# Sparse attention, first half of the queries: float32 weights and values in place of high and low parts

## Chip, cores and metric

One core of a Trainium2 chip runs the whole kernel as one program. The metric is the device time of one execution in microseconds (us). The time of a kernel is the median of its runs.

## The reference, cut to what is touched

The reference is two transformer layers over 1024 tokens of width 1024. Layer 0 mixes with gated linear attention and latent attention, layer 1 with a sparse attention and a state-space model (S5); each layer ends in a squared-ReLU network. The change touches the last lines of the sparse attention:

```python
def _dsa(q, k, v, q_idx, k_idx, w_idx):        # 8 heads of 64, 1024 tokens
    ...
    def one_block(args):                        # 128 queries at a time
        ...
        _, sel = lax.top_k(score, topk)         # 256 keys for each query
        sel_ok = sel <= qpos[None, :, None]
        ...
        s = jnp.where(sel_ok[:, None], s, -jnp.inf)
        p = jax.nn.softmax(s, axis=-1)
        return jnp.einsum('bhqk,bqkhd->bhqd', p, v_sel)
```

The kernel computes it densely: a bias row of 0 or a large negative number (`bias[qb]`) takes out the keys that are not chosen, and the weights `p` of all keys up to the query are multiplied with the values.

## The kernel before, in words

**Order of the work.** The kernel is written as a plain sequence of operations (`program`, line 2161) that a planner, `Plan`, records and then orders itself. `Plan.order` (line 242) is a list scheduler with its own table of costs (`cost`, line 207): at each moment it gives each free engine the ready operation with the smallest key, where the key is the place in the written sequence less a number called `rush`. It also places all SBUF and PSUM tiles. The result is a fixed order for each engine. Every instruction has line 471 in the profile, so it is told apart by its tiles. A changed operation anywhere can change the order of everything that is planned at about the same time or later.

**High and low parts.** Most products are made of operands that are split in two: `split` (line 580) writes a rounded copy (type `fp32r`, the high part) by a ScalarE copy, and the rest (low part) by a subtraction on VectorE or GpSimd. `mm3` then multiplies high by high, high by low and low by high. `fp32r` operands are multiplied in one pass. Some small products of the kernel are multiplied in plain float32.

**The layer around the change.** After the network of layer 0 the program calls, woven into each other: the index scores and the search for the 256th largest score (`index`, `topk`, lines 1587 and 1616, VectorE and ScalarE), the projections of layer 1 (`l1_in`, line 1699, TensorE), the S5 (`s5`, all engines), and the sparse attention `dsa` (line 1753) for the first 512 queries (h = 0) and then for the last 512 (h = 1). After them come the output projection and the network, dense work for TensorE.

**Values.** In `l1_in` eight tiles of 128 tokens by 512 value columns are made in PSUM. Each is split, for each of two groups of four heads, into a tile in which a head has 128 columns, high and low part beside each other: for an even head high first, for an odd head low first. So 4 ScalarE copies of 128 columns and 4 VectorE subtractions a tile, and two writes to the DRAM buffer `dv`. `dsa` loads those it needs back through GpSimd's queue: for h = 0 four tiles for each group of heads.

**Weights times values.** `attention` (line 1015) goes through heads and pairs of query blocks. `first` makes the scores, and exponentials in `p` with ScalarE. `second` takes pairs of key blocks (`kb`): up to four 128x128 transposes of `p` into one PSUM tile `pt`, a ScalarE copy to `hi` (tile `pth`), a VectorE subtraction to `lo` (tile `ptl`), and four matmuls into the accumulator:

```python
v = value(kb + a)                     # 128 columns: high and low part of one head
TE.matmul(o, v, hi[:, c], ...)        # c: 256 query columns
TE.matmul(o, v, lo[:, c], ...)
```

On the diagonal (`kb == qa`) the quarter that lies above it is cleared in both tiles by a memset (VectorE here, `ZE = 1`) and not transposed. The accumulator then has 128 rows: 64 from the values' high part, 64 from their low part. `fold` (line 1083) adds the two: a ScalarE copy of one half to the rows of the other (tile `fold`), and a VectorE addition into `og`. For h = 0 a head has three pairs of key blocks, two of them on the diagonal. The latent attention of layer 0 uses the same two functions.

Of the kernel before, what the change touches and what calls it, by code (L numbers as in the profile page):

```python
# [11 lines left out]
F32 = mybir.dt.float32  # L12
# [504 lines left out]
class Kern:  # L517
# [497 lines left out]
    def attention(self, items):  # L1015
# [27 lines left out]
        def second(i, pr, pp):  # L1043
            hd, h, _, _, value, emit = items[i]
            qa = h * 4 + pr * 2
            if pr == 0:
                acc[i] = self.ps1()
            o = acc[i][:, pr * 256:pr * 256 + 256]
            for kb in range(0, qa + 2, 2):
                self.nc.rush += self.DS  # L1050

                pt = self.ps1((P, 2, 2, P))
                hi, lo = self.slab(F32R, "pth"), self.slab(F32R, "ptl")
                off = P if kb == qa else 0
                for z in (hi, lo):
                    if off:
                        (self.ZE or G).memset(z[:, :off].bitcast(F32), 0.0)
                        self.nc.after(pp[2])
                for a in range(2):
                    for j in range(2):  # L1060
                        if kb + a <= qa + j:
                            TE.transpose(pt[:, 1 - a, j, :], pp[j][:, (kb + a) * P:(kb + a + 1) * P], self.identf)
                self.split(pt.rearrange("p a b c -> p (a b c)")[:, off:], hi[:, off:], lo[:, off:], S, V)
                for a in range(2):
                    v = value(kb + a)
                    c = slice(256 - a * 256, 512 - a * 256)
                    TE.matmul(o, v, hi[:, c], start=kb + a == 0, stop=False)
                    TE.matmul(o, v, lo[:, c], start=False, stop=kb + a == qa + 1)
                self.nc.rush -= self.DS
            if pr == 1:  # L1070
                emit(acc.pop(i), sums[hd // 2, h])
# [11 lines left out]
    def fold(self, po, odd, og, sums):  # L1083
# [4 lines left out]
        tmp = self.slab(name="fold")  # L1088
        self.copy(self.S, tmp[own], po[other])
        V.tensor_tensor(og[own], po[own], tmp[own], ALU.add)  # L1090
# [608 lines left out]
    def l1_in(self, x, dq, dk, dv, du):  # L1699
# [4 lines left out]
        for b in range(8):  # L1704
# [3 lines left out]
            for hg in range(2):  # L1708
# [6 lines left out]
                nc.scalar.dma_start(out=dv[b, hg], in_=v.rearrange("p a b c -> p (a b c)").bitcast(F32))  # L1715
# [37 lines left out]
    def dsa(self, dq, dk, dv, bias, mix, h):  # L1753
# [3 lines left out]
        ld = G.dma_start  # L1757

        def load(pr):

            if pr % 2 == 0:
                for b in range(4 * h + 4):
                    v = self.slab(F32R, "vv")
                    ld(out=v, in_=dv[b, pr // 2])
                    val[pr // 2, b] = v
# [9 lines left out]
        def item(hd):  # L1775
# [19 lines left out]
            def emit(po, sums):  # L1795
                if not odd:
                    og[h] = self.slab(name="og")
                self.fold(po, odd, og[h], sums)
# [6 lines left out]
            return hd, h, prep, score, lambda kb: val[hd // 4, kb][:, (hd % 4) * P:(hd % 4 + 1) * P], emit  # L1805

        yield from self.attention([item(hd) for hd in range(8)])
# [327 lines left out]
BY = {'unit_h': 'S', 'unit_l': 'E', 'loadx_h': 'S', 'loadx_l': 'V', 'glao_h': 'S', 'glao_l': 'G', 'mlac_h': 'S', 'mlac_l': 'V', 'mlaq_h': 'S', 'mlaq_l': 'G', 'mlao_h': 'S', 'mlao_l': 'E', 'half_h': 'S', 'half_l': 'V', 'fc1_h': 'S', 'fc1_l': 'E', 'dsao_h': 'S', 'dsao_l': 'G', 'x2_h': 'H', 'x2_l': 'V', 'y_h': 'H', 'y_l': 'G', 'glu_h': 'H', 'glu_l': 'V', 'lnacc': 'G', 'lnsq': 'G', 'gla': 'G', 'gdl': 'G', 'gor': 'G', 's5u': 'V', 's5a': 'G', 's5m': 'G', 's5n': 'G', 's5t': 'G', 's5g': 'G', 'lo16': 'V', 'hi16': 'V'}  # L2135
BACK, SQUARE = 1, 1   
# [24 lines left out]
def program(K, A, out, stop=None):  # L2161
# [23 lines left out]
    dv = K.dram("dv", [8, 2, P, N])  # L2185
# [211 lines left out]
```

## Time and profile before

| what | value |
|---|---|
| median of 3 runs | 2381.92 us (2379.25 to 2382.75) |
| profiled execution, its own time | 2390.38 us |
| span in that profile | 2388.6 us, 33377 instructions |
| busy: TensorE / weight loads / VectorE / ScalarE / GpSimd | 2305.8 / 1910.2 / 1768.3 / 1330.8 / 468.2 us |
| mean granted TensorE clock | 0.99 |

How to read it: PE is TensorE's matmuls and PEld its weight loads, DVE is VectorE, ACT is ScalarE, POOL is GpSimd, SP only issues DMAs. A matmul's form is given as rows*columns of the weights and the shape of the moving operand; a plain float32 matmul leaves two such records. A record lasts from its issue until its results are out, and the next one starts before that, so the step from start to start is what it costs an engine that has enough to do.

### The profile page before, as it was taken

To read this page: it belongs to the slowest core of one execution; us is meant where nothing else is said; L and a number is where in the kernel's file an instruction comes from. 1 tells how busy PE (TensorE), PEld (TensorE's weight loads), DVE (VectorE), ACT (ScalarE), POOL (GpSimd) and SP (SyncE) were. 2 spreads that over 40 slices of the span, in tenths; PEclk is the share of its full clock that TensorE was granted. 3 is DMA by queue.
4 is the path that set the end of the run, shared out by engine and by line. 5 is a ranking of instruction groups with operands and counts; after the bars stand their busy time and mean duration, and the time that the engine had idled before them with its cause. 6 is when DMAs were issued, how large, how long until landed. Compare 5 with 4: busy or idle time off the path is not lost. (4 is left out here: it accounts for less than half of the span.)

```text
span 2388.6 us, 33377 instructions
## 1 busy us (share of the span) xinstructions
PE 2305.8 (97%) x11368; PEld 1910.2 (80%) x11368; DVE 1768.3 (74%) x3353; ACT 1330.8 (56%) x2648; POOL 468.2 (20%) x488
## 2 busy tenths in 40 slices
PE   8999999999999999999999997899999999999997
PEld 7788888887878788887778876788877787888887
DVE  8676778468776567579799989885587755675796
ACT  4365567437555554446578775775275455444463
POOL 1252332232000000003211235752320000000021
PEclk9999999999999999999999998999999999999998
DMA  5420001325654585655103469553155546665561
GB/s 182 170 80 1 1 1 51 101 71 162 204 168 154 190 299 194 207 189 203 67 36 115 145 204 282 155 157 127 53 166 187 168 146 212 225 253 193 178 238 36
DMA packets 174939, 356.59 MB, mean 149 GB/s; under 512 B 26784, under 2 KB 39344, under 8 KB 174768
## 3 DMA queue, kind: packets, MB, share of 16 engines
q1 hardware_dynamic: 110704, 243.81, 31.9%
q10 hardware_dynamic: 51392, 87.58, 9.9%
q0 software_dynamic: 12672, 23.07, 3.6%
q8 instruction: 89, 1.46, 0.3%
q14 instruction: 82, 0.67, 0.1%
HBM read 249.66 MB, written 104.73 MB: 148 GB/s over the span
## 5 line engine op out<-in xcount | busy, mean ns | idle before, releaser
L471 PE MATMUL PS<-bh,wb 128*128 128x512 f32 x1792 | 569.0, 395 | 14.5 <-ACT u L471 6.8
L471 PEld LDWEIGHTS PS<-bh,wb 128*128 128x128 f32 x1792 | 335.6, 188 | 105.1 <-ACT u L471 12.6
L471 PE MATMUL PS<-bl,wb 128*128 128x512 f32 x896 | 350.5, 391 | 0.0
L471 PE MATMUL PS<-gl,vh 128*128 128x512 f32 x832 | 324.0, 390 | 2.1 <-DVE gl L471 2.1
L471 PE MATMUL PS<-gh,vh 128*128 128x512 f32 x832 | 322.6, 391 | 2.5 <-ACT vh L471 1.8
L471 PE MATMUL PS<-gh,vl 128*128 128x512 f32 x832 | 323.7, 390 | 0.0
L471 PEld LDWEIGHTS PS<-bl,wb 128*128 128x128 f32 x896 | 169.2, 189 | 34.1
L471 PEld LDWEIGHTS PS<-gh,vh 128*128 128x128 f32 x832 | 156.1, 188 | 37.5 <-ACT vh L471 2.2
L471 PEld LDWEIGHTS PS<-gl,vh 128*128 128x128 f32 x832 | 156.2, 188 | 35.2 <-DVE gl L471 2.5
L471 PEld LDWEIGHTS PS<-gh,vl 128*128 128x128 f32 x832 | 156.2, 188 | 32.3
L471 POOL TENSOR_TENSOR wl<-wr,wh 128x512 fp32r<-128x512 f32 x77 | 120.8, 1584 | 254.9 <-ACT wh L471 154.4
L471 ACT ACTIVATE c<-c 128x512 f32<-128x512 f32 x224 | 140.7, 630 | 50.5 <-DVE c L471 43.5
L471 PE MATMUL PS<-xh,wh 128*128 128x512 f32 (+1 forms) x400 | 155.2, 393 | 12.7 <-ACT xh L471 6.7
L471 POOL TENSOR_TENSOR lnacc<-res,res 128x512 f32<-128x512 f32 (+1 forms) x8 | 9.8, 1223 | 768.1 <-DVE res L471 740.9
L471 ACT ACTIVATE gh<-hr 128x512 fp32r<-128x512 f32 x208 | 129.2, 623 | 52.1 <-PE PS L471 32.6
L471 PE MATMUL PS<-xh,wl 128*128 128x512 f32 (+1 forms) x400 | 154.1, 388 | 2.8 <-POOL wl L471 2.8
L471 DVE TENSOR_TENSOR gl<-hr,gh 128x512 fp32r<-128x512 f32 x208 | 147.7, 711 | 10.9 <-PE PS L471 5.2
L471 PE MATMUL PS<-xl,wh 128*128 128x512 f32 (+1 forms) x400 | 155.3, 389 | 0.0
L471 ACT ACTIVATE wb<-wf 128x512 fp32r<-128x512 f32 x96 | 59.7, 628 | 153.2 <-DMA wf<-in_l_w 94.0
L471 DVE TENSOR_TENSOR wb<-s,wb 128x512 fp32r<-128x512 f32 x128 | 87.8, 688 | 77.0 <-ACT wb L471 76.9
L471 DVE TENSOR_TENSOR vl<-s,vh 128x512 fp32r<-128x512 f32 x112 | 84.2, 754 | 78.5 <-ACT vh L471 39.9
L471 ACT ACTIVATE vh<-s 128x512 fp32r<-128x512 f32 x112 | 70.2, 629 | 108.3 <-PE PS L471 73.2
(371 smaller groups left out, 5497.5 us busy)
## 6 DMA issues: line engine op xcount, KB each, us to landing
wr<-in_l_w SPq DMA_DIRECT2D x118, 512.0 KB, 5.3
hr<-hd SPq DMA_DIRECT2D x208, 256.0 KB, 3.4
wf<-in_l_w SPq DMA_DIRECT2D x80, 512.0 KB, 3.8
hd<-t ACTq DMA_DIRECT2D x128, 256.0 KB, 2.7
hd<-c ACTq DMA_DIRECT2D x96, 256.0 KB, 2.3
wr<-in_l_fm SPq DMA_DIRECT2D x25, 512.0 KB, 5.3
wr<-in_l_wo SPq DMA_DIRECT2D x16, 512.0 KB, 4.5
dx<-res ACTq DMA_DIRECT2D x32, 256.0 KB, 2.4
```

The source lines that it names most:

```text
L471: r = getattr(queue.real, method)(*a, **k)
```

## The change

For the first half of the queries (`PLAIN = 0,`) the weights are copied once to a float32 tile and multiplied with float32 values of 64 columns. The accumulator uses only the head's own 64 rows, so that `fold` is one copy. On the diagonal nothing is cleared; the second matmul covers only the 128 columns below. The value tiles of the first four token blocks are written a second time, whole and in float32; `dv` gets another shape. The second half and the latent attention of layer 0 stay as they are.

```diff
--- before.py
+++ after.py
@@ -1012,7 +1012,8 @@
         output(*late)
-    def attention(self, items):
+    def attention(self, items, plain=False):
+
@@ -1046,20 +1047,28 @@
             if pr == 0:
                 acc[i] = self.ps1()
             o = acc[i][:, pr * 256:pr * 256 + 256]
+            if plain:
+                o = o[64 * (hd % 2):64 * (hd % 2) + 64]
             for kb in range(0, qa + 2, 2):
                 self.nc.rush += self.DS
                 pt = self.ps1((P, 2, 2, P))
-                hi, lo = self.slab(F32R, "pth"), self.slab(F32R, "ptl")
+                hi, lo = (self.slab(name="pt"), None) if plain else (self.slab(F32R, "pth"), self.slab(F32R, "ptl"))
                 off = P if kb == qa else 0
                 for z in (hi, lo):
-                    if off:
+                    if off and not plain:
                         (self.ZE or G).memset(z[:, :off].bitcast(F32), 0.0)
                         self.nc.after(pp[2])
                 for a in range(2):
                     for j in range(2):
                         if kb + a <= qa + j:
                             TE.transpose(pt[:, 1 - a, j, :], pp[j][:, (kb + a) * P:(kb + a + 1) * P], self.identf)
+                if plain:
+                    self.copy(S, hi[:, off:], pt.rearrange("p a b c -> p (a b c)")[:, off:])
+                    TE.matmul(o, value(kb), hi[:, 256:], start=kb == 0, stop=kb == qa)
+                    TE.matmul(o[:, off:], value(kb + 1), hi[:, off:256], start=False, stop=kb == qa, skip_group_check=off > 0)
+                    self.nc.rush -= self.DS
+                    continue
                 self.split(pt.rearrange("p a b c -> p (a b c)")[:, off:], hi[:, off:], lo[:, off:], S, V)
                 for a in range(2):
                     v = value(kb + a)
@@ -1080,14 +1089,17 @@
             ahead = nxt
             yield
-    def fold(self, po, odd, og, sums):
+    def fold(self, po, odd, og, sums, plain=False):
         V = self.V
         own, other = (slice(64, 128), slice(0, 64)) if odd else (slice(0, 64), slice(64, 128))
-        tmp = self.slab(name="fold")
-        self.copy(self.S, tmp[own], po[other])
-        V.tensor_tensor(og[own], po[own], tmp[own], ALU.add)
+        if plain:
+            self.copy(self.S, og[own], po[own])
+        else:
+            tmp = self.slab(name="fold")
+            self.copy(self.S, tmp[own], po[other])
+            V.tensor_tensor(og[own], po[own], tmp[own], ALU.add)
         if odd:
             V.reciprocal(sums, sums)
             rs, ps = self.slab(name="rs", shape=(P, 8, 64)), self.ps1()
@@ -1705,14 +1717,18 @@
             ps = self.ps1((P, 8, 64))
             bs = slice((b % 4) * P, (b % 4 + 1) * P)
             self.tm(us, lambda k: tuple(t[:, bs] for t in x[k][b // 4]), ps)
-            for hg in range(2):
+            if 1 in PLAIN or 0 in PLAIN and b < 4:
+                v = self.slab(name="vv")
+                self.copy(S, v, ps.rearrange("p a b -> p (a b)"))
+                nc.scalar.dma_start(out=dv[2, b], in_=v)
+            for hg in range(2 if len(PLAIN) < 2 and (b < 4 or 1 not in PLAIN) else 0):
                 v = self.slab(F32R, "vv", (P, 4, 2, 64))
                 for par in range(2):
                     src = ps[:, hg * 4 + par:hg * 4 + 4:2, :]
                     hs, ls = v[:, par::2, par, :], v[:, par::2, 1 - par, :]
                     self.copy(S, hs, src)
                     V.tensor_tensor(ls, src, hs, ALU.subtract)
-                nc.scalar.dma_start(out=dv[b, hg], in_=v.rearrange("p a b c -> p (a b c)").bitcast(F32))
+                nc.scalar.dma_start(out=dv[hg, b], in_=v.rearrange("p a b c -> p (a b c)").bitcast(F32))
             yield
         us = [self.unit(A["l1_u"][i]) for i in range(4)]
         for h in range(2):
@@ -1754,14 +1770,18 @@
         V, S, G, TE = self.V, self.S, self.G, self.TE
         val, qk, og = {}, {}, {}
-        ld = G.dma_start
+        ld, plain = G.dma_start, h in PLAIN
         def load(pr):
-            if pr % 2 == 0:
+            if plain and pr == 0:
+                for b in range(4 * h + 4):
+                    val[b] = self.slab(name="vv")
+                    ld(out=val[b], in_=dv[2, b])
+            elif not plain and pr % 2 == 0:
                 for b in range(4 * h + 4):
                     v = self.slab(F32R, "vv")
-                    ld(out=v, in_=dv[b, pr // 2])
+                    ld(out=v, in_=dv[pr // 2, b])
                     val[pr // 2, b] = v
             for odd in range(2):
                 q = self.slab(F32R, "qa")
@@ -1795,16 +1815,19 @@
             def emit(po, sums):
                 if not odd:
                     og[h] = self.slab(name="og")
-                self.fold(po, odd, og[h], sums)
+                self.fold(po, odd, og[h], sums, plain)
                 if odd:
                     self.dump("o_dsa", og[h], (pr, slice(None), slice(h * N, h * N + N)))
                     hi, lo = self.slab(F32R, "mh"), self.slab(F32R, "ml")
                     self.split(og[h], hi, lo, self.by("dsao_h"), self.by("dsao_l"))
                     mix[pr][h] = (hi, lo)
-            return hd, h, prep, score, lambda kb: val[hd // 4, kb][:, (hd % 4) * P:(hd % 4 + 1) * P], emit
-
-        yield from self.attention([item(hd) for hd in range(8)])
+            def value(kb):
+                return val[kb][:, hd * 64:hd * 64 + 64] if plain else val[hd // 4, kb][:, (hd % 4) * P:(hd % 4 + 1) * P]
+
+            return hd, h, prep, score, value, emit
+
+        yield from self.attention([item(hd) for hd in range(8)], plain)
     def turn(self, a, n):
@@ -2133,6 +2156,7 @@
+PLAIN = 0,
 BACK, SQUARE = 1, 1
 EARLY, ER = 100, 2
 FIRST = 3
@@ -2182,7 +2206,7 @@
     dr = K.dram("dr", [KD, P, T])
     dq = K.dram("dq", [4, 2, 2, P, N])
     dk = K.dram("dk", [4, 2, 2, 2, P, N])
-    dv = K.dram("dv", [8, 2, P, N])
+    dv = K.dram("dv", [3, 8, P, N])
     du = K.dram("du", [4, 2, P, N])
```

## Rows read from the trace of the kernel before

**Rows 1.** The page, part 1: busy time of TensorE and VectorE.
```profile
PE 2305.8 (97%) x11368; PEld 1910.2 (80%) x11368; DVE 1768.3 (74%) x3353; ACT 1330.8 (56%) x2648; POOL 468.2 (20%) x488
```

**Rows 2.** Busy time by stage, with the columns in the first row.
```profile
core 0: us, PE busy (x) PEld busy (x) DVE busy (x) ACT busy (x) POOL busy (x), PEclk, DMA share, GB/s
...
1250.00:1290.00 40.00, 38.46 (x170) 31.31 (x169) 39.58 (x94) 27.83 (x66) 5.15 (x4) 1.00 0.26 93
...
1467.00:1540.00 73.00, 61.66 (x403) 51.53 (x401) 65.58 (x186) 57.71 (x141) 53.34 (x62) 0.95 0.67 186
1540.00:1645.00 105.00, 102.62 (x661) 89.50 (x661) 95.63 (x242) 88.02 (x170) 49.97 (x58) 1.00 0.57 166
2089.00:2149.00 60.00, 60.00 (x267) 49.67 (x266) 45.39 (x71) 27.62 (x48) 4.54 (x3) 1.00 0.68 254
```

**Rows 3.** Matmuls from 2089 to 2149, by form: busy us, mean ns of one.
```profile
L471 PE MATMUL PS<-gl,vh 128*128 128x512 f32 x89 | 34.6, 389 | 0.0
```

**Rows 4.** TensorE in order of time, steps from start to start, from 1502 to 1506.
```profile
1502.34 0.39 PE L471 MATMUL PS<-s5T,s5U 128*128 128x128 f32 x2
1502.56 0.39 PE L471 MATMUL PS<-s5tab,s5x 128*128 128x128 f32 x2
...
1505.04 0.28 PE L471 MATMUL PS<-ptl,vv 128*128 128x256 f32 x1
1505.16 0.29 PE L471 MATMUL PS<-pth,vv 128*128 128x256 f32 x1
1505.28 0.28 PE L471 MATMUL PS<-ptl,vv 128*128 128x256 f32 x1
```

**Rows 5.** Matmuls from 1467 to 1540, by form.
```profile
L471 PE MATMUL PS<-ident,p 128*128 128x128 f32 x91 | 17.8, 299 | 4.2 <-ACT p L471 3.9
...
L471 PE MATMUL PS<-pth,vv 128*128 128x256 f32 x48 | 14.7, 319 | 3.8 <-DVE pth L471 1.8 <-DVE ptl L471 0.9 <-DVE SM L471 0.6
L471 PE MATMUL PS<-s5T,s5U 128*128 128x128 f32 x32 | 6.4, 289 | 0.0
L471 PE MATMUL PS<-ka,qa 128*128 128x512 f32 x14 | 6.2, 441 | 0.2 <-DVE SM L471 0.2
```

**Rows 6.** What TensorE and ScalarE waited for, 1467 to 1540: us, times, longest.
```profile
PE PS L471 <- ACT p L471: 3.9, 7, 1.1
PE PS L471 <- DVE ptl L471: 3.5, 8, 1.2
PE PS L471 <- DVE pth L471: 1.8, 2, 1.1
...
ACT p L471 <- DVE SM L471: 6.1, 7, 2.8
```

**Rows 7.** VectorE from 1467 to 1540, by form.
```profile
L471 DVE TENSOR_TENSOR ptl<-PS,pth 128x384 fp32r<-128x384 f32 x16 | 8.4, 523 | 0.3 <-ACT pth L471 0.3
...
L471 DVE TENSOR_TENSOR ptl<-PS,pth 128x512 fp32r<-128x512 f32 x8 | 5.5, 684 | 1.0 <-ACT pth L471 1.0
L471 DVE TENSOR_TENSOR og<-PS,fold 64x512 f32<-64x512 f32 x8 | 5.4, 680 | 2.0 <-ACT fold L471 1.8
...
L471 DVE MEMSET pth<- 128x128 f32 x18 | 3.0, 165 | 0.0
L471 DVE MEMSET ptl<- 128x128 f32 x18 | 3.0, 165 | 0.8 <-PE PS L471 0.8
```

**Rows 8.** TensorE in order of time: matmuls with 64 columns of weights.
```profile
253.85 0.67 PE L471 MATMUL PS<-v,ket 64*64 64x128 f32 x14
...
305.10 0.39 PE L471 MATMUL PS<-cl,wh 128*64 128x512 f32 x1
305.32 0.39 PE L471 MATMUL PS<-ch,wl 128*64 128x512 f32 x1
305.55 0.39 PE L471 MATMUL PS<-ch,wh 128*64 128x512 f32 x1
```

**Rows 9.** Tiles vv and v: ns, min/median/max, first and last start; then the eighth write.
```profile
L471 ACT ACTIVATE vv<-PS x96: 202/250/325, 217.2 to 1322.0; 128x64 fp32r<-128x64 f32 x64, 128x128 fp32r<-128x128 f32 x32
...
L471 POOL DMA_DIRECT2D vv<-dv x24: 527/535/762, 1435.5 to 1569.5; - x24
L471 ACTq DMA_DIRECT2D dv<-vv x16: 326/327/743, 1254.4 to 1324.4; - x16
...
L471 ACT ACTIVATE v<-PS x8: 595/598/602, 80.5 to 127.0; 128x512 f32<-128x512 f32 x8
...
1292.18 0.33 ACTq L471 DMA_DIRECT2D dv<-vv  x1
```

## The prediction, made before the change was run

> **What bounds the kernel now.** Part 1 of the page comes first: TensorE is busy for 97% of the span, VectorE for 74% [rows 1]. A busy TensorE is not a full one here, so I read the busy time by stage next. From 2089 to 2149, in the last network, TensorE issues 267 matmuls of 512 columns in 60.00 us [rows 2, 3]: 0.225 us each, while one lasts 389 ns. That step from start to start is the real price of a matmul. In the order of time the same step is 0.12 us for 256 columns of fp32r and, for a plain float32 matmul of 128 columns, 0.22 us for its two records, 0.11 each [rows 4].
>
> With these steps I add up what TensorE has to do where the changed code runs. All 48 matmuls each of `pth` and `ptl` of the first half lie between 1467 and 1540 us; the second half and what is woven into it go on to 1645. In the first stretch the window counts 403 records [rows 2, 5]: 233 transposes and float32 records of 128 columns at 0.11 us (the 91 of `p`, the 32 of `s5T` and others like them) make 25.6 us, 126 of 256 columns at 0.12 (`pth`, `ptl`, 30 scores) 15.1, 16 of 384 at 0.17 (between the two) 2.7, and 28 of 512 (`ka` 14, `kl` 14) 6.3. The sum is 49.7 of 73 us, so TensorE has 23.3 us to spare, although it shows as busy for 61.66. In the next stretch the same sum over its 661 records gives 96.9 of 105 us, which is 92%.
>
> So the first half of the sparse attention is not TensorE's. VectorE is busy for 65.58 of the 73 us, ScalarE for 57.71, GpSimd for 53.34 [rows 2]. VectorE is the fullest, and what TensorE waits for comes through it: directly from `ptl` and `pth`, 3.5 and 1.8 us, and from the exponentials `p`, 3.9 us, which themselves wait 6.1 us for the row minimum that VectorE computes [rows 6]. The granted clock in this stretch has a mean of 0.95, against 1.00 in the next one: TensorE had gaps before it fell.
>
> **The change, part by part.** *VectorE loses* in the first half: 16 subtractions of 384 columns, 8.4 us, and 8 of 512, 5.5 us; 8 additions in `fold`, 5.4 us; and 32 of the 36 memsets in the window (two for each of 16 diagonal pairs; the other four belong to the second half), 32/36 of 6.0 us, 5.3 us [rows 7]. Together 24.6 us, so that 41.0 of its 65.6 remain.
>
> *TensorE gains.* Each of the 24 key pairs had four matmuls of 256 columns, 4 x 0.12 = 0.48 us, 11.5 us in all. Now a pair off the diagonal (8 of them) has two float32 matmuls of 256 columns, 2 x 0.44 = 0.88 us by twice the step of the 128-column pair; one on the diagonal (16) has 0.44 + 0.22 = 0.66 us. That is 7.0 + 10.6 = 17.6 us, or 6.1 us more: 49.7 becomes 55.8. No float32 matmul with 128 rows and 64 columns of weights is in the trace. An fp32r one with 64 columns is, and its step, 0.22 to 0.23 us for 512, is that of 128 columns [rows 8], so I take no discount for the narrow weights. From below the bound is 3 us less than now (see the third rival), from above 6.1.
>
> *ScalarE* keeps its copy out of `pt`, and the one in `fold` now writes `og` itself: nothing changes there. It gains four copies of a whole value tile, 0.60 us each by the row of `v`, and four writes to `dv` at 0.33 us of its queue [rows 9]: 3.7 us. Only token blocks 0 to 3 are concerned, whose splits end with the eighth write, at 1292 [rows 9]; from 1250 to 1290 ScalarE is busy for 27.83 of 40 us [rows 2], which is the cover. Without it they would cost up to 3.7 us, since the search for the threshold runs through the same queue; they could not gain anything. I take 0.5. The split of all eight tiles stays, as the second half needs it: nothing is saved there.
>
> *GpSimd* issues four value loads fewer, at 0.54 us [rows 9]: 2.2 us, behind which the loads of queries and keys queue. The bounds are 0 and 2.2 us gained; I take 0, as TensorE's list of waits names no such load in this stretch. The other shape of `dv` moves nothing.
>
> *What is late next.* A step's chain was transpose, ScalarE copy, VectorE subtraction, matmuls; the subtraction drops out, and VectorE's queue no longer delays the minima. With 41.0 us for VectorE, 57.7 for ScalarE, 55.8 for TensorE and 51 for GpSimd no engine is full, and ScalarE and TensorE are the next. If TensorE reaches the 92% of the following stretch, the stage takes 55.8 / 0.92 = 60.6 us and gains 12.4. If ScalarE can be filled only as there, 88.02 of 105 or 84%, it takes 57.7 / 0.84 = 68.7 and gains 4.3. I take the middle, 8.4, and add 0.9, as S5 work that now waits for a place can move between the two stretches. The ends are 4.3 and, with TensorE without a gap, 17.2.
>
> **Sum:** 9.3 less in the stage and 0.5 more in the projections is 8.8 us less. After 1645 the work is TensorE's, unchanged, and only starts earlier. The profiled execution's own time is 2390.38 us (span 2388.6), so it would be 2381.6; the median of the runs is 8.5 us lower, 2381.92, and by the same difference I forecast 2373.1.
>
> **The rivals.** *First, hidden:* the gaps are latencies of a chain through transposes, ScalarE and PSUM, and VectorE's load only looks like their cause. Then only the waits that name `ptl` or `pth` go, 3.5 + 1.8 = 5.3 us, and the 6.1 us of TensorE's new work eat them: 0.8 us more, 2382.7. For it speaks that the waits at `p` are put down to ScalarE; against it that VectorE is at 90%, and that the exponentials themselves wait 6.1 us for it [rows 6].
>
> *Second, slower:* TensorE pays for the four passes in full. If its order leaves the same 23.3 us of gaps between other instructions, the 24 longer groups of matmuls lengthen the stage by 6.1 us: 2388.0. It decides as soon as the gaps filled are fewer than 6.1 us of 23.3. Against it speaks that the removed subtractions stand in front of the very matmuls that get longer.
>
> *Third, side by side:* the 14 float32 records with 64 rows and 64 columns of weights, whose places in the array alternate, run in 0.67 us [rows 8], some 0.03 us from start to start instead of 0.11. Matmuls of an even head (rows 0 to 63 of the accumulator) and an odd one (64 to 127) use different columns of the array too, and if the order puts them next to each other, the new 17.6 us shrink towards 8.8: 3 us less than now. The stage then comes near ScalarE's floor of 57.7 us: 15 us less, 2367. Against it: within a step all matmuls use the same half, and such neighbours run one after another in the trace (the fp32r steps of 0.23 us [rows 8]). The Trainium skill states the rule (TensorE: Matmul & The Clock Gate, section on packing small matmuls): matmuls whose tiles lie in different column groups of the array run concurrently. By that rule the price would be at the low end wherever two heads meet in the order; this trace agrees for the alternating 64-column tiles, at 0.03 us.
>
> *That the change does not do what it says:* the planner makes a new order for everything from the projections on, and S5 work may be put where it hurts. No row prices that; it is why the range reaches beyond the forecast's own ends.
>
> **How the numbers follow.** Forecast 0.60, hidden 0.20, slower 0.11, side by side 0.09. A measurement of this kernel tells some 0.2% from no change, 4.8 us: faster is below 2377.1, slower above 2386.7. The forecast's near end, 4.3 gained less 0.5, just misses that, so 0.03 of it goes to "same": faster 0.57 + 0.09 = 0.66, same 0.20 + 0.03 = 0.23, slower 0.11. The range goes from TensorE without a gap and the loads' 2.2 us as well, 2381.9 - 19.4 = 2362, to the hidden case with the value copies at their upper bound, 2381.9 + 0.8 + 3.7 = 2386. The slower case and larger surprises of the new order are left out.
>
> **What would show it.** Right: the stage with the first half's transposed weights is 6 to 12 us shorter, VectorE is busy there for about 41 us, the new matmuls leave 96 records with steps near 0.22 us (256 columns) and 0.11 (128), and from the output projection on all is as before, but earlier. Wrong: the stage keeps about 73 us with VectorE idle (hidden), TensorE gets fuller by 6 us and the stage longer (slower), records of even and odd heads start within 0.05 us of each other (side by side), or the stage gains and the projections before it or the second half give it back.

## The result, and the profile after

The changed kernel takes 2397.8 us (median of 10 runs), the kernel before beside it on the same chip 2382.8 (10 runs). The ratio is 1.0056, 95% interval [1.0037, 1.0074]: slower by 13 us, where 9 us less were forecast. One of the ten runs, the profiled one, had a granted clock of 0.75 and took 2862.7 us; the ratio is that of the means of the others, and the lines here are of a second profile of the same kernel (label a0_changed: 2398.0 us, ratio 1.0068 [1.0054, 1.0082], span 2393.9).

Part 1 of its page, to be set beside [rows 1]:

```profile
PE 2312.6 (97%) x11368; PEld 1913.4 (80%) x11368; DVE 1755.6 (73%) x3294; ACT 1330.4 (56%) x2649; POOL 460.9 (19%) x482
```

TensorE has 6.8 us more, near the forecast's 6.1; VectorE has only 12.7 us less, though 24.6 were taken away from it; more on both below.

To see where the time went I cut both traces at events, not at times: the start of the last copy of an index score (`ir<-PS`, ScalarE), the first score of the sparse attention (`p<-PS,SM`, VectorE), and the 8th and 16th ScalarE copy out of an accumulator (`fold` or `og`), which end the first and the second half. So there are three stretches: search and projections, first half, second half. The kernel before, with the columns of [rows 2]:

```profile
1281.00:1467.00 186.00, 171.96 (x784) 148.09 (x783) 169.77 (x384) 128.44 (x323) 63.50 (x58) 0.97 0.64 192
1467.00:1533.00 66.00, 54.66 (x349) 45.32 (x348) 60.44 (x171) 51.54 (x129) 48.74 (x54) 0.95 0.67 185
1533.00:1643.50 110.50, 108.12 (x709) 94.51 (x708) 99.34 (x255) 93.60 (x181) 54.56 (x66) 1.00 0.58 170
```

The changed kernel:

```profile
1278.10:1472.80 194.70, 173.59 (x783) 150.69 (x782) 172.50 (x390) 128.29 (x323) 59.85 (x57) 0.94 0.61 184
1472.80:1532.20 59.40, 56.73 (x343) 42.45 (x342) 38.92 (x98) 49.41 (x128) 39.95 (x47) 0.97 0.67 185
1532.20:1648.30 116.10, 110.12 (x716) 97.12 (x717) 104.43 (x263) 93.28 (x179) 59.25 (x68) 0.99 0.54 160
```

The second column is the length. The first half is 6.6 us shorter, and VectorE, third of the busy times, has 38.92 us of work there and no longer 60.44. But search and projections are 8.7 us longer and the second half 5.6: 7.7 us more in all, in stretches whose arithmetic the change hardly touches. The two halves together go only from 176.5 to 175.5 us: the first half now holds less of the work that is woven into it (GpSimd is busy there for 39.95 us and no longer 48.74, and the four loads that are gone are 2.2 of that by [rows 9]), and the second half holds more. These are lengths of one trace each. What TensorE waited for in the first half is nearly gone; of the lines of [rows 6] these took the place:

```profile
PE PS L471 <- ACT pt L471: 1.5, 1, 1.5
PE PS L471 <- ACT s5U L471: 0.8, 2, 0.5
PE PS L471 <- ACT og L471: 0.2, 1, 0.2
```

The new matmuls are the 96 records forecast, in one line of the list of forms, here under the tile `pt`:

```profile
L471 PE MATMUL PS<-pt,vv x96: 272/379/431, 1476.9 to 1531.9; 128*64 128x256 f32 x64, 128*64 128x128 f32 x32
```

In the order of time, a run of 12 of them (8 of 256 columns, 4 of 128):

```profile
1504.59 2.12 PE L471 MATMUL PS<-pt,vv 128*64 128x256 f32 x12
1506.64 0.39 PE L471 MATMUL PS<-ka,qa 128*128 128x256 f32 x1
```

From the first start to that of the next instruction are 2.05 us; the forecast's steps, 8 x 0.22 + 4 x 0.11, give 2.20.

What made search and projections longer shows first at VectorE, which in that stretch has 2.7 us more to do and 6.0 us more idle time. Its waits before (1281 to 1465):

```profile
DVE wl L471 <- ACT wh L471: 2.7, 1, 2.7
...
DVE SM L471 <- ACT ja L471: 1.6, 4, 0.6
```

After (1278 to 1471):

```profile
DVE SM L471 <- ACT ja L471: 7.3, 9, 3.2
DVE qkl L471 <- ACT qkh L471: 4.5, 3, 2.2
DVE wl L471 <- ACT wh L471: 3.6, 3, 1.8
```

`ja` are ScalarE's counts for the search and `qkh` its copies of queries and keys. The changed kernel's order puts them later against VectorE's, and all of VectorE's waits that the list names sum to 20.3 us in place of 13.5. TensorE's longest wait of the stretch is for `qkl`, the low parts of queries or keys, which VectorE writes only after its last passes of the search. First the kernel before (1430 to 1480), then the changed one (1440 to 1490):

```profile
PE PS L471 <- DVE qkl L471: 2.0, 2, 1.3
PE PS L471 <- DVE qkl L471: 9.6, 2, 9.1
```

TensorE has another gap early in the search. Busy time in 10 us at the same place in the search, before:

```profile
1301.00:1311.00 10.00, 9.86 (x42) 9.55 (x41) 9.83 (x38) 9.88 (x31) 0.00 (x0) 1.00 0.21 79
```

And after:

```profile
1298.10:1308.10 10.00, 6.11 (x16) 4.76 (x16) 9.68 (x35) 9.97 (x31) 1.28 (x1) 0.73 0.14 52
```

16 matmuls in place of 42, at a granted clock of 0.73. The changed kernel in the order of time:

```profile
1300.95 0.40 PE L471 MATMUL PS<-wh,xh 128*128 128x512 f32 x1
1301.19 0.39 PE L471 MATMUL PS<-wl,xh 128*128 128x512 f32 x1
1303.77 1.24 PE L471 MATMUL PS<-wh,xh 128*128 128x512 f32 x2 [2.19 <-ACT wh L471]
1304.81 0.63 PE L471 MATMUL PS<-wh,xl 128*128 128x512 f32 x1
1305.24 0.63 PE L471 MATMUL PS<-wh,xh 128*128 128x512 f32 x1
```

One conversion of weights (`wh`) stood on ScalarE behind passes of the search. TensorE waited 1.7 us for a split of values and then 2.2 us for it, and when it went on its step was 0.43 us (1304.81 to 1305.24) and not 0.24 (1300.95 to 1301.19): the lower of the two clock levels (the granted clock from 1304.4 to 1309 is 0.50). How much of the 8.7 us this gap made is not shown by this trace: a second kernel below, with the value copies alone, has the same order as the changed one up to 1408 us, and in its trace the same 10 us hold 25 matmuls at a clock of 0.83, and the way to that point is some 4 us shorter.

### The profile page after: what moved, and what is told of

The parts are those of the page before. It is cut to its first block, busy times and chain, and to the rows that moved or that the text cites. A ratio compares the mean times of both kernels' runs of the same rounds, so it can differ in the third digit from the quotient of the medians.

```text
span 2860.9 us, 33317 instructions
## 1 busy us (share of the span) xinstructions
PE 2814.6 (98%) x11368; PEld 2078.2 (73%) x11368; DVE 1761.7 (62%) x3294; ACT 1344.6 (47%) x2649; POOL 451.9 (16%) x482
## 5 line engine op out<-in xcount | busy, mean ns | idle before, releaser
L471 PE MATMUL PS<-bh,wb 128*128 128x512 f32 x1792 | 670.2, 456 | 3.1 <-ACT u L471 2.8
L471 PEld LDWEIGHTS PS<-bh,wb 128*128 128x128 f32 x1792 | 357.4, 200 | 158.8 <-ACT u L471 5.1
L471 PE MATMUL PS<-bl,wb 128*128 128x512 f32 x896 | 410.6, 458 | 0.0
L471 PE MATMUL PS<-gl,vh 128*128 128x512 f32 x832 | 381.0, 458 | 1.8 <-DVE gl L471 1.8
L471 PE MATMUL PS<-gh,vl 128*128 128x512 f32 x832 | 378.8, 456 | 0.0
L471 PE MATMUL PS<-gh,vh 128*128 128x512 f32 x832 | 377.5, 457 | 0.0
L471 PE MATMUL PS<-xh,wh 128*128 128x512 f32 (+1 forms) x400 | 178.8, 452 | 12.0 <-ACT xh L471 6.3
L471 PE MATMUL PS<-xl,wh 128*128 128x512 f32 (+1 forms) x400 | 179.8, 450 | 0.0
L471 PE MATMUL PS<-xh,wl 128*128 128x512 f32 (+1 forms) x400 | 177.7, 447 | 0.0
L471 DVE TENSOR_TENSOR c<-PS,u 128x512 f32<-128x512 f32 x96 | 66.3, 691 | 146.0 <-PE PS L471 100.1
```

Source lines behind the costliest of these rows:

```text
L471: r = getattr(queue.real, method)(*a, **k)
```

## The experiments

Three theories stood at the start. **N**: the loss is the newly made order, not the change. **P**: the float32 passes cost more than VectorE's relief gives. The **forecast's reasoning**: VectorE bounds the first half, so its relief is what counts. Later **C** came in, that the extra value copies delay the search, and **R**, that the loss is the change's own in any order.

### The changed kernel again, and its parts in the order of before

The first four kernels ran together (the kernel before: 2384.5 us). In three of them, and in a fourth later, every instruction keeps the place that the planner gave it for the kernel before; only when the order is issued is an operation dropped or replaced:

```diff
         for i in order:
             queue, method, a, k = self.ops[i][:4]
+            if i in self.swap:
+                if self.swap[i] is None:
+                    continue
+                queue, method, a, k = self.swap[i]
```

`instead()` marks the last operation for dropping, `instead(queue, method, ...)` for replacing. The changed kernel, as it is:

> The changed kernel itself, for a trace in which the clock is not held down. Theory N (new order): the planner has ordered everything from the projections on anew, and the loss of some 13 us comes from there. Then the stretch with the 96 float32 records is about as long as before or shorter (73 us or less by the same marks), and the time is lost in the projections and the search before it or in the second half. Theory P (passes): TensorE's 6.1 us of float32 passes are not absorbed; then that stretch itself is 6 us or more longer, and the rest is as before. Time: 2397, 13 us above the kernel before.

Measured: 2398.0 us, 1.0068 [1.0054, 1.0082]. The loss stands.

**The attention part alone, order kept**:

```diff
-                    TE.matmul(o, v, hi[:, c], start=kb + a == 0, stop=False)
-                    TE.matmul(o, v, lo[:, c], start=False, stop=kb + a == qa + 1)
+                    TE.matmul(o, v, hi[:, c], start=kb + a == 0, stop=False)
+                    self.nc.instead(TE, "matmul", po[:, b:], v[:, r:r + 64].bitcast(F32), ...)
+                    TE.matmul(o, v, lo[:, c], start=False, stop=kb + a == qa + 1)
+                    self.nc.instead()
```

and likewise nothing in place of the memsets, the subtraction and the addition in `fold`; the ScalarE copy out of `pt` writes plain float32.

> The attention part of the change alone, with the order of before held: the planner plans the old operations, and at issue the subtraction, the memsets, two of four matmuls and the addition in fold are left out, and the other two matmuls are float32 with 64 columns of values (high parts only: the values' low parts are left out). Theory N: the parts themselves gain or cost nothing, so 0 to 9 us less than before. Theory P: about 6 us more than before. My forecast's reasoning, that VectorE bounds the stage: 4 to 9 us less.

Measured: 2388.9 us, 1.0018 [1.0005, 1.0032].

**VectorE's relief alone, order kept** (TensorE keeps its four fp32r matmuls, all on the weights' high part). Against the kernel just shown:

```diff
-                    self.nc.instead()
+                    self.nc.instead(TE, "matmul", o, v, hi[:, c], start=False, stop=kb + a == qa + 1)
```

> Order of before held, VectorE's work of the first half taken away alone: no subtractions, half the memsets, no addition in fold (24.6 us less 2.6), and TensorE keeps its four fp32r matmuls, all on the high part (the products with the weights' low part are replaced). If VectorE bounds the stage as forecast: 8 to 12 us less than before. If its load only looks like the cause: within 3 us of before.

Measured: 2383.9 us, 0.9998 [0.9985, 1.0011]: in the total nothing, which is what was expected if VectorE's load only looks like the cause.

**The passes alone, order kept** (VectorE does all its work of before). Against the attention part alone:

```diff
                 V.tensor_tensor(lo[:, off:], flat[:, off:], hi[:, off:], ALU.subtract)
-                if plain:
-                    self.nc.instead()
```

and the memsets and the addition in `fold` are kept in the same way.

> Order of before held, TensorE's price alone: the two float32 matmuls in place of four fp32r ones, while VectorE still does all its subtractions, memsets and additions (the values' low parts are left out and fold adds a copy of the same rows). Theory P: 6 us more than before. If TensorE has room, as forecast: 0 to 2 us more. Theory N says the same as the forecast here.

Measured: 2387.9 us, 1.0021 [1.0010, 1.0032].

**The whole change, order kept**: the attention part as above, the four value copies and writes issued ahead of the splits, and each load of `vv` replaced by one of a whole value tile.

```diff
+            if b < 4 and self.spare is not None:
+                self.nc.first[len(self.nc.ops)] = [
+                    (S, "activation", (self.spare, ps.rearrange("p a b -> p (a b)"), AF.Copy), {}),
+                    (nc.scalar, "dma_start", (), dict(out=dw[b], in_=self.spare))]
...
                     ld(out=v, in_=dv[b, pr // 2])
+                    if h == 0:
+                        self.nc.instead(G, "dma_start", out=v.bitcast(F32), in_=self.dram("dw", [4, P, N])[b])
```

> The whole change (whole value tiles copied, written and loaded; float32 weights; no subtraction, memset or addition in fold), but with every instruction at the place that the order of before gives it; eight loads of whole value tiles instead of four. Theory N (the loss is the newly made order): what is left is the passes, +4 us as with the order kept before, and at most 1 to 2 us for the copies: 2388 to 2390 us where before has 2384.5, ratio 1.0015 to 1.003; the stretch from the last index score to the first half keeps 186 to 188 us. Theory C (the four copies and writes on ScalarE themselves delay the search): that stretch takes 194 us as in the changed kernel, about 2397 us, ratio 1.005 or more. Theory P (the passes alone): the same as N without the copies, 2388.5.

Measured: 2389.4 us, 1.0023 [1.0013, 1.0032]. The stretch ahead of the first half does not take the 194 us of theory C:

```profile
1279.70:1461.70 182.00, 169.90 (x784) 146.46 (x782) 168.00 (x384) 128.52 (x323) 65.44 (x58) 0.99 0.64 195
```

The first half in the traces of these four (columns as above). The attention part alone:

```profile
1467.10:1535.30 68.20, 62.01 (x348) 40.62 (x347) 39.78 (x107) 50.78 (x128) 48.86 (x53) 1.00 0.64 177
```

VectorE's relief alone:

```profile
1465.40:1527.40 62.00, 52.37 (x349) 42.97 (x348) 43.63 (x123) 50.45 (x129) 49.55 (x53) 0.97 0.72 196
```

The passes alone:

```profile
1458.80:1529.10 70.30, 61.85 (x349) 40.91 (x348) 60.82 (x171) 51.89 (x129) 48.31 (x54) 1.00 0.65 174
```

The whole change:

```profile
1461.70:1530.00 68.30, 62.98 (x348) 41.38 (x347) 40.80 (x107) 50.94 (x128) 48.86 (x53) 0.98 0.64 180
```

Against the 66.0 us of before, VectorE's relief alone gives 4.0 back, the passes alone cost 4.3, and the whole change costs 2.3 with VectorE busy for 40.80 of 68.30 us. Why a kept order makes so little of the relief was not tried further; the obvious reading is that what stood behind a subtraction starts earlier, but nothing moves into the gap. In the total the whole change costs 5.3 us (2389.4 less 2384.2, the kernel before beside it) and the attention part 4.3, which leaves 1.0 for the copies, with intervals that overlap. So C falls, P holds in a fixed order, and 8 us of the 13 are still missing: they come with the order.

### Newly made orders

**The value copies alone, planned anew**, **the attention part alone, planned anew**, and **the kernel before in another order**. The first leaves `dsa` as it was, the second leaves out the copies and takes the values from their high parts:

```diff
-        ld, plain = G.dma_start, h in PLAIN
+        ld, plain = G.dma_start, False
```
```diff
-                v = self.slab(name="vv")
-                self.copy(S, v, ps.rearrange("p a b -> p (a b)"))
-                nc.scalar.dma_start(out=dv[2, b], in_=v)
```

The third changes one constant of the kernel before, the planner's reckoning of the time from an instruction's end to its release of the next:

```diff
-    WAIT = 45
+    WAIT = 46
```

It stands in no instruction; it only shifts what the planner takes to be ready first. With the order the planner also chooses the places of the tiles and, for some operations, one of two engines; below, "order" stands for all of this.

> Value copies and writes alone (dv with its new shape), the attention as before; the planner makes its own order. The arithmetic of before is all done. Theory N: a new order, so any time from 6 us below to 12 above before, and the difference lies in stretches that the copies do not touch as well. Theory C: 7 to 9 us more, all of it between the last index score and the first half of the sparse attention, 2392 to 2394. Theory P and the forecast's reasoning: 0 to 1 us more, 2385.

Measured: 2398.4 us, 1.0060 [1.0044, 1.0075].

> The attention part alone, planned anew: float32 matmuls with 64 columns, no subtraction, memset or addition in fold in the first half; no whole value tiles are written (the values' low parts are left out of the product). Theory N: a new order, any time from 6 us below to 12 above before; the first half itself about 7 us shorter as in the changed kernel, since the planner uses VectorE's relief. Theory P: 4 us more, 2388.5. Theory C: without the copies no loss before the first half, so that its gain of 6.6 us reaches the end: 2378. The forecast's reasoning: 9 us less, 2375.5.

Measured: 2395.5 us, 1.0051 [1.0037, 1.0064].

> The kernel before with one constant of the planner's reckoning changed (WAIT 46 in place of 45): the same instructions, all of them, in another order. Theory N: the time moves by 4 us or more, in either direction, with single stages moved by as much as in the changed kernel (the search stretch or the second half by 5 us). Theories C and P and the forecast's reasoning: nothing of what they price is touched, 2384.5 within 2 us.

Measured: 2396.5 us, 1.0049 [1.0036, 1.0061].

The third is the decisive one: the same operations as before, all of them, and 12 us more. (Not quite the same instructions: a few operations went to another engine. VectorE has 3358 records and not 3353, GpSimd 483 and not 488.) The total moved as theory N had it, the single stages did not: 185.5, 66.3 and 113.0 us are within 2.5 of before, so most of the 12 us lies outside these three. Four copies alone give as much as the whole change, though with the order kept they cost about 1. And the stretches that lengthen are not the same: with the copies alone, search and projections keep their 186.5 us and the first half takes 70.7; with the attention part alone they keep 183.4, the first half takes 56.5, and the second half 124.6.

That left a choice. Either every new order costs some 10 us against a good old one, or orders simply scatter, or (R) the changed kernel's loss is its own.

> The kernel before, unchanged, as a control: every theory expects no difference, ratio 1.000 with an interval that holds 1, and a second trace of the order of before. What its stages differ from the first trace by is how far two traces of one kernel scatter: 1 to 3 us each.

Measured: 2384.5 us, 0.9990 [0.9979, 1.0001]. Its three stretches are 186.4, 65.9 and 110.4 us, within 0.4 of the first trace, while the spans were 2383.5 and 2388.6. That is better than stretches repeat in general: with the order kept the search has the same work in all traces but for the four copies, and took 186.9 (attention part), 187.2 (relief), 182.7 (passes) and 182.0 us (whole change). A difference of up to 5 us in the search of two single traces is within scatter.

> The kernel before with WAIT 44: the same instructions, a third order. Theory N as it stands after the first other order (the order of before is a good one among many, and any newly made order costs about 10 us): 2391 to 2400 us. Rival theory R (the first other order was an unlucky one, a newly made order costs nothing on average, and the changed kernel's loss is its own): 2384 us within 4.

Measured: 2402.7 us, 1.0069 [1.0055, 1.0082]. That is above both ranges.

> The changed kernel with WAIT 44. Theory N: the changed kernel with another newly made order lies where the kernel before with a newly made order lies, 2391 to 2400 us, within 5 us of the kernel before with WAIT 44. Theory R: the loss is the change's own, 2396 to 2400 us, and 10 us or more above the kernel before with WAIT 44. The forecast's reasoning, if the orders are alike but for the change: 9 us below the kernel before with WAIT 44.

Measured: 2405.7 us, 1.0078 [1.0065, 1.0090]. Within 5 us of the kernel before with WAIT 44, as N asks, though above its range; against R, which asked for 10 more.

> The changed kernel with WAIT 46, to be set beside the kernel before with WAIT 46 (2396.5 us, 1.0049). Theory N: 2391 to 2400 us, within 5 us of that one. Theory R (the change costs what it cost at 45, 13 us, in any order): 2408 us. Passes alone, no gain from VectorE's relief in any order: 2400. The forecast's reasoning: 2388.

Measured: 2386.7 us, 1.0003 [0.9993, 1.0014]. That is 9.7 us less than the kernel before with WAIT 46: neither N's 2391 to 2400 nor R's 2408, but the forecast's 2388. R falls, and N as "every new order costs 10 us" falls with it. What is left is scatter: the orders move either kernel by up to 18 or 19 us.

> The kernel before with WAIT 47, a fourth order. So far the kernel before took 2384.5, 2402.7 and 2396.5 us in three orders, the changed kernel 2398.0, 2405.7 and 2386.7. Theory O (the order decides, each order moves either kernel by about 8 us): 2384 to 2405 us. No theory narrows it further.

Measured: 2402.5 us, 1.0074 [1.0053, 1.0095], within theory O's range.

> The changed kernel with WAIT 47. Theory O: 2384 to 2406 us, and its difference to the kernel before with WAIT 47 anywhere from 13 us more to 10 us less, as in the three pairs so far. If the passes were the whole of the change's cost in any order: 4 us more than that one. The forecast's reasoning in any order: 9 us less.

Measured: 2394.9 us, 1.0045 [1.0028, 1.0063], 7.5 us less than the kernel before with WAIT 47: within theory O's range, and not the passes' 4 us more.

The four pairs in one view (medians; the kernel before at 45 as it stood beside the changed one; at 46 the two stood beside different runs of the kernel before, 2384.2 and 2385.6; stretches of one trace each, whose run lay up to 6 us from its kernel's median):

| WAIT | before, us | changed, us | difference | search, first, second half before | changed |
|---|---|---|---|---|---|
| 44 | 2402.7 | 2405.7 | +3.0 | 183.6, 63.6, 116.7 | 198.3, 56.8, 117.5 |
| 45 | 2384.5 | 2398.0 | +13.5 | 186.0, 66.0, 110.5 | 194.7, 59.4, 116.1 |
| 46 | 2396.5 | 2386.7 | -9.7 | 185.5, 66.3, 113.0 | 179.0, 59.0, 119.2 |
| 47 | 2402.5 | 2394.9 | -7.5 | 186.2, 63.2, 115.0 | 193.4, 64.6, 114.3 |

The mean difference is -0.2 us, with a standard error of 5.3 (the four scatter by 10.7): over these orders the change is worth nothing that can be told from the scatter, and four pairs are too few to exclude the 9 us less of the forecast or as much more. The kernel before at WAIT 45 is the fastest of its four by 12 us, and the change was set beside that one. In three of four pairs the first half is 6.6 to 7.3 us shorter, as forecast. The two halves together, though, change by -6.0, -1.0, -1.1 and +0.7 us (WAIT 44 to 47): only at 44 is most of that gain left at the end of the second half. And the search takes 193.4 to 198.3 us in three orders of the changed kernel and 179.0 in the fourth, where no other order here goes beyond 187.2 (four of the kernel before, and the two parts planned anew). Whether the planner tends to lay the changed kernel's search worse, or three draws fell badly, these runs do not tell.

The scatter of the kernel before is not that of the same stretch either. Its three stretches sum to 362.5 to 364.8 us in all four orders; most of its 12 to 18 us lies outside of them. WAIT remakes the order from early on (VectorE's departs from that of before at 37, 553 and 228 us for WAIT 44, 46 and 47), the change only from 1245. What compares like with like is the pair at one WAIT: its two orders agree up to about 1245 us.

The changed kernel's good order (WAIT 46), with the same cuts:

```profile
1280.70:1459.70 179.00, 167.46 (x786) 146.21 (x786) 168.12 (x382) 126.65 (x319) 61.27 (x56) 0.99 0.67 198
1459.70:1518.70 59.00, 56.81 (x342) 42.11 (x340) 37.60 (x101) 50.29 (x128) 41.65 (x46) 0.97 0.73 200
1518.70:1637.90 119.20, 112.01 (x718) 99.15 (x718) 105.14 (x260) 91.95 (x179) 59.96 (x70) 0.96 0.53 155
```

Its VectorE waits less in the search, above all for ScalarE's counts:

```profile
DVE s5yt L471 <- ACT s5g L471: 2.8, 1, 2.8
DVE SM L471 <- ACT ja L471: 2.2, 4, 1.0
```

The first half is the one of WAIT 45 (59.0 and 59.4), but the search takes 179.0 us and not 194.7, at a granted clock of 0.99 and not 0.94. The long wait for `qkl` is there too (6.4 us in place of 9.1), so it alone does not make the difference. These 15.7 us, between two orders of the same operations, are more than the whole effect that was forecast.

### One gap closed by hand

In the changed kernel, three conversions of weights are issued some 50 to 80 places earlier than planned:

```diff
+EARLIER = (9915, 9750), (9917, 9799), (9920, 10058)
...
+        for i, j in EARLIER:
+            order.remove(i)
+            order.insert(order.index(j), i)
```

> The changed kernel in its own order, with three conversions of weights (wh<-wr of the u projection) some 50 to 80 places earlier, so that they no longer stand behind several passes of the search on ScalarE. In the changed kernel TensorE waits 1.7 and 2.2 us around them and then runs 14 matmuls with a step of 0.43 in place of 0.23 us. Theory G (this gap is what the newly made order costs before the first half): 3.9 us of waits and 2.8 us of slow matmuls come back, 6.7 us in all: 2391 us, ratio 1.0028, no 10 us window with fewer than 35 matmuls between the last index score and the end of the u projection. Theory S (the search on VectorE ends that stretch, TensorE only waits in another place): the gap goes, the bias is ready no earlier, and TensorE idles longer ahead of the first half: 2397 us, within 2.

Measured: 2397.8 us, 1.0057 [1.0038, 1.0076], against 2398.0 for the changed kernel: no gain. The gap is only half closed:

```profile
1298.00:1308.00 10.00, 7.31 (x25) 6.28 (x24) 9.28 (x35) 9.17 (x28) 1.26 (x1) 0.83 0.21 79
```

25 matmuls in place of 16, but not the 35 that theory G asked for: the wait for `wh` is gone from this place, that for `vv` has grown to 2.7 us, and another for `wh`, some 40 us later, is 2.9 us where it was 2.4. Even these 25 need not come from the edit: the trace of the value copies alone, with the same order up to there and no conversion moved, has 25 in this place as well. In this trace the stretch is 190.9 us, 3.8 shorter, and the last bias comes as much earlier, which S denied; that is within the scatter of the search, the median does not show it, and the span, 2396.6, is longer by 2.7 than that of the changed kernel. TensorE's wait for `qkl` at the end of the search is as long as ever, 9.2 us. G's ratio, 1.0028, lies outside the interval, but the gap it speaks of was not closed, so G is not refuted in full; S is not shown. Moving these three conversions gains nothing that can be seen.

## Why the prediction was wrong

**What VectorE loses: right, within 3 us.** 24.6 us were forecast. With the order kept, VectorE's busy time falls by 21.9 us on the whole page (1746.4 against 1768.3), in the first half from 60.44 to 40.80 us, and in the changed kernel to 38.92. The planner then gave part of it back: of the three stretches' 329.55 us before, 306.93 are left with the order kept, but 315.85 in the new order, in which GpSimd's sum is 159.04 and no longer 168.93 (order kept). Several operations may run on either of two engines, and VectorE has 3294 records in the new order and 3289 in the kept one, GpSimd 482 and 488; the rest of the difference was not traced.

**What TensorE gains: right.** 6.1 us forecast. The steps are as forecast (0.22 us for 256 columns, 0.11 for 128), and the passes alone cost 4.3 us in the stage and 3.4 in the total (2387.9 less 2384.5). That the busy time of the whole page is 6.8 us up is no proof: between orders of the kernel before it moves as much (2305.8 to 2317.1), and in the changed kernel's order of WAIT 46 it is 2305.5.

**The copies: right.** 0.5 forecast, about 1 measured with the order kept, below what the intervals can tell. Of the four loads fewer on GpSimd nothing can be said: the kept order has all eight.

**The stage: right for the first half in the new order, wrong for what it was to give.** 9.3 us less were forecast between ends of 4.3 and 17.2. The first half became 6.6 us shorter (6.8 and 7.3 at WAIT 44 and 46, 1.4 longer at 47). ScalarE, which the forecast's low end took as the limit at 84%, is busy for 49.41 of 59.4 us, or 83%. But the forecast let only 0.9 us of work move between this stretch and the next; both together are 1.0 us shorter, not 6.6. With the order kept the stage is 2.3 us longer, and the relief alone, which should have shown VectorE as the limit by 8 to 12 us, gives 4.0 in the stage and nothing in the total.

**The sum: wrong.** The step that failed is the sum itself, "9.3 less in the stage and 0.5 more in the projections is 8.8 us less": it takes the stage's gain to the end, allows the projections 0.5 us and the second half nothing, and so has everything around the first half keep its order and its time. It did not: search and projections took 8.7 us more in the trace, the second half 5.6, against 6.6 gained. (What it says of the time after 1645 holds: from the 16th copy to the end the changed kernel takes 745.6 us, the kernels with the order of before 741 to 748.) The shares are shown by the kept order: the whole change in the order of before costs 5.3 us, the new order the other 8. That a new order is made was told, as the last of the rivals ("No row prices that"), but it was given no chance: forecast, hidden, slower and side by side filled 1.00. Its price, as the kernel before shows, is 17.1, 12.3 and 18.0 us for WAIT 44, 46 and 47, each against the order of before beside it: up to twice the forecast effect, though for an order remade from early on and not only from 1245 us. The order of before is at the good end of that scatter, which a single trace can't tell. The range ended at 2386 for the same reason; only 1 of the 4 orders of the changed kernel comes within a microsecond of it. The last of the signs that the prediction named for being wrong, "the stage gains and the projections before it or the second half give it back", is what the changed kernel's trace shows.

**The rivals.** *Slower*, with 6.1 us more and 2388.0, is near what happens when the order is kept: 5.3 us more, 2389.4, though only 2.3 of them in the stage. Its condition, that the order leaves the same gaps between other instructions, is just what a kept order means. *Hidden* is not settled: with the order kept, 4.0 us of relief and 4.3 of passes are near its 5.3 and 6.1, and the relief alone changed nothing in the total; against it stands the first half in three of four new orders, 7 us shorter although TensorE has more to do, but with less work woven into it. *Side by side* is right in its mechanism and too rare to count. In the run of 12 records shown above the kernel's order goes from head 4 to head 5, and at that one place of the 96 the records interleave: the odd head's first starts at 1505.85, before the even head's last two at 1505.94 and 1506.05, which accounts for the 2.05 us in place of 2.20. In the order of WAIT 46 two such records of 256 columns start 0.02 us apart, at 1485.92 and 1485.94. So the price is at the low end where two heads meet, as the prediction had it; this order lets them meet once, for about 0.15 us.

**What stays open.** The medians differ by 13.5 us, the two traces by 5.3 (2393.9 less 2388.6), and the three stretches by 7.7; of the rest no more can be said, as traces of one and the same order differ by as much outside of them. Why one order's search waits more for ScalarE than another's was read from the waits, not tried beyond the one gap. What the change is worth in the mean over orders is open: -0.2 us with a standard error of 5.3. No kernel that beats both was found: the best of the changed ones is equal to the kernel before, 1.0003 [0.9993, 1.0014].

## What to carry to other kernels

Where a planner makes the order, an edit is two changes: what it does, and a new draw of the order. Measure them apart: issue the edit in the old order, and run the kernel without the edit in two or three other orders, before a row is given a price. If the draw scatters by more than the edit is worth, as here (18 us against 9), compare means over orders, more than the four pairs taken here, or search over orders for both kernels alike; a kernel whose order happens to be a good one, as here, will make most edits look bad. And add up the neighbours of the stretch that got shorter: a planner can shorten it by moving work out of it.

## What the runs showed that was not expected

One or two steps of one planning constant, which no instruction carries, are worth up to 18 us of 2384, or 0.75%, with the same operations.

TensorE's clock fell less with the float32 passes: 0.98 to 1.00 in the first half with the passes and the order kept (61.85 to 62.98 us busy), 0.95 before (54.66 us busy), 0.97 with the relief alone (52.37). That part of the price of the passes is paid back in this way is an estimate from these rows, not a measurement.

Half the weight columns save nothing in the step of a float32 matmul among its own head's (0.22 us for 256 columns), but records of the accumulator's two halves can run beside each other where they meet (0.02 to 0.09 us apart), without anything laid out for it. The weight load gets shorter too: 136 ns in the mean for 64 columns, 188 for 128 columns in the last network of the same trace.
